# A softmax router on one core: eight-row loads in place of four-row loads for rows 4 to 35, and one float32 load for the first four rows

## The chip, the cores and the metric

The kernel runs on one core of a Trainium2 chip. The time is device microseconds of one execution; the time before is the median of seven runs. One further execution was taken by the hardware profiler, and every duration below comes from that one unless a text says otherwise.

## What is computed

```python
batch, seq, dim = 16, 512, 1024
num_loras = 8
# x: (16, 512, 1024) float32, router_weights: (1024, 8) float32
def reference(x, router_weights):
    logits = np.matmul(x, router_weights)
    exp_logits = np.exp(logits - np.max(logits, axis=-1, keepdims=True))
    return (exp_logits / np.sum(exp_logits, axis=-1, keepdims=True)).astype(np.float32)
```

There are 8,192 tokens. Each is multiplied by a 1024 x 8 matrix, and a softmax over eight numbers follows. The input is 33.6 MB, the output 0.26 MB.

## The kernel before, in words

The 8,192 tokens are laid over 128 partitions so that partition p holds 64 consecutive tokens (line 25 of the listing that follows). One "row" of the kernel is the j-th token of every partition: 128 tokens, 4 KB of float32 each. The 64 rows are worked off in order, and all of them stay in one bfloat16 buffer, `x_all` (`xa`), which has room for everything; no load waits for a buffer.

**Loads.** Rows 0 to 3 come as float32 into `x_f32` through SyncE's queue: two loads of two rows (line 134), each with a semaphore of its own, `s_f[0]` and `s_f[1]`. Rows 4 to 62 come through GpSimd's queue, which casts to bfloat16 on the way (line 185). The list `LOADS` (line 40) gives the rows of each: the first 4 is the float32 part, then twelve loads of four rows, three of two, five of one. The last row comes in three pieces of 4, 2 and 2 chunks of 128 columns (line 198). A load lays each partition's rows down as one contiguous run, so its packets hold one partition's rows: 16 KB of float32 read and 8 KB of bfloat16 written for four rows. GpSimd issues all of them at the start, one behind the other, and builds an identity matrix and a filler tile after the second (line 188). ScalarE's queue brings the weights (line 140).

**Handing rows on.** SyncE waits for the loads in order and counts their rows up in the semaphore `s_in` (lines 167 to 173). So a load's rows are available all at once, when the whole load is there.

**Work on one row.** TensorE transposes the row's eight 128 x 128 chunks against the identity into PSUM (line 293; the first row's at 248), five into `ptv` and three into `pts`. VectorE copies the five to SBUF (line 410), ScalarE the three (line 366). TensorE multiplies the chunks with the weights into `lg` (line 280). The loop (TensorE's bodies `rows_multiply` and `rows_turn`) turns row j + 1 before it multiplies row j, and puts two filler matmuls of 512 columns into every second row. Every eight rows VectorE and ScalarE do the softmax for a group (lines 430 to 452, 355).

**Start.** ScalarE waits for `s_f[0]`, casts rows 0 and 1 (`cast`, line 349), copies chunks for these rows, then waits for `s_f[1]`, casts rows 2 and 3 and copies their chunks. An activation table is loaded ahead of the first cast.

**End.** The last rows stand alone: rows 60 to 62 come out of single-row loads, row 63 in pieces (line 326), and after the last multiplication (line 340) follow one maximum, one exponential, a sum, a reciprocal, a scaling and the second output store (line 178). The first output store (line 176) goes out while the last pieces are still worked on.

Of the kernel before, what the change touches and what calls it, by code (L numbers as in the profile page):

```python
# [11 lines left out]
def kernel(  # L12
# [6 lines left out]
    nc = tc.nc  # L19
# [9 lines left out]
    x_rows = x.rearrange("b s d -> (b s) d").rearrange("(p j) d -> p j d", p=P)  # L29
# [7 lines left out]

    LOADS = [4] * 13 + [2, 2, 2] + [1] * 5  # L40
    PIECES = [4, 2, 2]
    G, SKIP = 8, 4
    TRIPS = 31
# [5 lines left out]
    DONE = ends[-2]  # L49
    assert sum(LOADS) == J - 1 and sum(PIECES) == KO and ends[-1] == J - ALONE  # L50
    VN, SN = 5, 3
# [3 lines left out]
    def sb(name, shape, dtype):  # L55
        size = mybir.dt.size(dtype)
        for n in shape[1:]:
            size *= n
        at = place[0]
        place[0] = -(-(at + size) // 64) * 64  # L60
        return nc.alloc_sbuf_tensor_at(name, shape, dtype, offset=at).ap()
# [5 lines left out]
    xa = sb("x_all", [P, J, D], bf16)  # L67
    x_f32 = sb("x_f32", [P, LOADS[0], D], fp32)
    identity = sb("identity", [P, P], bf16)
# [29 lines left out]
    sem = tc.alloc_semaphore  # L99


    s_f = [nc.alloc_semaphore(f"s_f{i}") for i in range(2)]
    s_w = nc.alloc_semaphore("s_w")
    s_ld = [sem(f"s_ld{i}") for i in range(len(LOADS))]
    s_z = [sem(f"s_z{i}") for i in range(len(PIECES))]
# [21 lines left out]

    first = [sum(LOADS[:i]) for i in range(len(LOADS))]
    cols = [sum(PIECES[:i]) for i in range(len(PIECES))]


    with tc.manual_schedule():
        early = [
            nc.sync.dma_start(
                out=x_f32[:, 2 * i:2 * i + 2, :], in_=x_rows[:, 2 * i:2 * i + 2, :]
            ).then_inc(s_f[i], 16)
            for i in range(2)
        ]
        early.append(
            nc.scalar.dma_start(  # L140
                out=w8, in_=router_weights.rearrange("(ko ki) n -> ko ki n", ko=KO)
            ).then_inc(s_w, 16)
        )
        for t in early:
            tc.no_tile_sem_insts.add(t.ins.name)
    tc.close()
# [19 lines left out]

    for j in range(LOADS[0]):
        sp.wait_ge(s_cast, j + 1)
        sp.sem_inc(s_in, 1)
    for i, r in enumerate(LOADS):  # L170
        if i:
# [11 lines left out]
    for i, r in enumerate(LOADS):  # L183
        if i:
            nc.gpsimd.dma_start(  # L185
                out=xa[:, first[i]:first[i] + r, :], in_=x_rows[:, first[i]:first[i] + r, :]
            ).then_inc(s_ld[i], 16)
        if i == 2:
# [3 lines left out]
                out=ident, in_=ident, compare_op=ALU.not_equal, fill=1.0, base=0,  # L192
# [154 lines left out]
    act = nc.scalar  # L347

    def cast(i):
        act.wait_ge(s_f[i], 16).then_inc(s_f[i], -16)  # L350
        for k in (2 * i, 2 * i + 1):
            act.copy(xa[:, k, :], x_f32[:, k, :]).then_inc(s_cast, 1)  # L352

# [9 lines left out]
    def act_copy(j, seen):  # L363

        act.wait_ge(s_ts, seen + 1)
        act.copy(xTs[j % 2], pts[j % 2][:, 0:SN, :]).then_inc(s_c[j % 2], 1)  # L366

    for i in range(2):
        cast(i)
        for j in (2 * i, 2 * i + 1):  # L370
            act_copy(j, j)
# [104 lines left out]
    with nc.body("dve_rows", valid_engines=only_dve):  # L476
# [42 lines left out]
        out=outv[:, J - ALONE:J, :], in0=ev3, in1=inv3.broadcast_to([P, ALONE, N]), op=ALU.mult  # L519
# [31 lines left out]
```

## Time and profile before

| | us |
|---|---|
| median of seven runs | 86.03 (85.86 to 86.48) |
| the profiled execution's own time | 85.89 |
| its span, first to last instruction | 84.6 |
| TensorE matmul busy | 63.2 (75%) |
| VectorE busy | 39.4 (47%) |
| ScalarE busy | 37.9 (45%) |
| DMA: bytes written | 18.12 MB, 3,904 packets |
| DMA: read from HBM | 33.59 MB, 400 GB/s over the span |
| GpSimd's queue, packets' time as a share of 16 engines' span | 91.0% |
| SyncE's queue, likewise | 7.5% |

The profile has a page of 40 equal slices (2.1 us each) with the busy share of each engine and of the DMA engines, a list of who waited for whom, the chain of work that ended last, a timeline of instructions, and tables by stretch. The trace under it also has a record for each DMA packet (start, duration, queue, bytes written) and for each landing (the sixteen semaphore increments of a load). "Busy" of a matmul is modelled and pipelined; queue engines (SPq, POOLq, PEq) are the sequencers that wait and issue. GB/s counts bytes written, so a float32-to-bfloat16 load at 215 GB/s reads 430 GB/s.

### The profile page before, as it was taken

How to read it: one execution, taken by the hardware profiler on the slowest of the kernel's cores; microseconds unless marked ns; L12 is line 12 of the kernel's file. 1: busy time of each engine (PE TensorE's matmuls, PEld its weight loads, DVE VectorE, ACT ScalarE, POOL GpSimd, SP SyncE). 2: the span in 40 equal slices, each digit the busy share in tenths (PEclk: the TensorE clock that was granted, in tenths of full speed). 3: DMA queues.
4: the chain of work that ended last, by engine and by line, in shares of the span. 5: the costliest groups of instructions: out<-in, count | busy, mean ns of one | idle time of the engine just before them, and what ended most of it. 6: DMA issues, size and time to landing. Idle time of an engine off the chain costs nothing. (4 is left out here: it accounts for less than half of the span.)

```text
span 84.6 us, 2926 instructions
## 1 busy us (share of the span) xinstructions
PE 63.2 (75%) x1094; PEld 51.9 (61%) x1094; DVE 39.4 (47%) x114; ACT 37.9 (45%) x81; POOL 13.4 (16%) x30
## 2 busy tenths in 40 slices
PE   0073759999895968959495986949497799999860
PEld 0043648888684747738384764837475588787650
DVE  0030422576472543834274452746256257665661
ACT  0049683366452442624254262535236246556470
POOL 0689999600000000000000000000000000000000
PEclk9999999999999999999999999999999999999998
DMA  5999999999999999999999999999999999999920
GB/s 107 417 426 260 221 202 225 205 229 205 213 217 213 221 213 221 205 229 205 221 213 221 209 225 202 232 202 225 205 225 190 215 217 213 201 210 208 180 102 23
DMA packets 3904, 18.12 MB, mean 214 GB/s; under 512 B 568, under 2 KB 1080, under 8 KB 2112
## 3 DMA queue, kind: packets, MB, share of 16 engines
q0 software_dynamic: 3312, 15.73, 91.0%
q1 hardware_dynamic: 576, 2.36, 7.5%
q10 hardware_dynamic: 16, 0.03, 0.1%
HBM read 33.59 MB, written 0.26 MB: 400 GB/s over the span
## 5 line engine op out<-in xcount | busy, mean ns | idle before, releaser
L366 ACT COPY xTs<-pts 128x384 bf16<-128x384 bf16 x63 | 30.0, 476 | 37.2 <-PE pts L293 36.8
L410 DVE COPY xTv<-ptv 128x640 bf16<-128x640 bf16 x63 | 30.9, 491 | 32.7 <-PE ptv L293 29.9
L293 PE MATMUL ptv<-identity,x_all 128*128 128x128 bf16 x311 | 28.5, 223 | 13.2 <-PEq L229 11.7
L293 PEld LDWEIGHTS ptv<-identity,x_all 128*128 (+1 forms) x311 | 18.7, 98 | 14.6 <-issue 14.5
L293 PE MATMUL pts<-identity,x_all 128*128 128x128 bf16 x186 | 21.3, 225 | 0.0
L280 PEld LDWEIGHTS lg<-w_bf,xTv 128*128 128x128 bf16 x305 | 15.5, 98 | 7.5 <-issue 0.8
L280 PE MATMUL spare<-filler 128*128 128x512 bf16 x61 | 19.2, 395 | 0.4
L280 PE MATMUL lg<-w_bf,xTv 128*128 128x8 bf16 x305 | 16.6, 167 | 0.0
L293 PEld LDWEIGHTS pts<-identity,x_all 128*128 x186 | 13.6, 101 | 0.0
L280 PE MATMUL lg<-w_bf,xTs 128*128 128x8 bf16 x183 | 13.2, 166 | 0.0
L185 POOL DMA_DIRECT2D x_all<-in_x_dram x20 | 10.7, 607 | 2.4 <-POOLq L147 2.4
L280 PEld LDWEIGHTS lg<-w_bf,xTs 128*128 128x128 bf16 x183 | 8.9, 96 | 0.0
L280 PEld LDWEIGHTS spare<-filler 128*128 128x128 bf16 x61 | 4.4, 101 | 2.5 <-issue 2.5
L287 PE MATMUL lg<-ident,w 8*128 8x8 f32 x8 | 1.0, 250 | 4.8 <-PEq L285 4.8
L352 ACT CAST x_all<-x_f 128x1024 bf16<-128x1024 f32 x4 | 4.0, 1045 | 0.0
L430 DVE TENSOR_REDUCE mx<-lg 128x8 f32 x8 | 1.8, 224 | 4.6 <-DVEq L480 4.1
L287 PEld LDWEIGHTS lg<-ident,w 8*128 8x128 f32 x8 | 0.9, 197 | 4.8 <-issue 4.8
L352 ACT ACT_TABLE_LOAD x1 | 1.3, 1283 | 5.3 <-ACTq L350 5.3
L355 ACT ACTIVATE ev<-ex 128x64 f32<-128x64 f32 x8 | 2.0, 256 | 1.6 <-DVE ex L430 0.9
L401 DVE CAST identity<-ident 128x128 bf16<-128x128 f32 x1 | 0.5, 518 | 4.8 <-POOL ident L191 4.8
L446 DVE TENSOR_REDUCE ssum<-ev 128x8 f32<-128x64 f32 x8 | 1.8, 220 | 0.1
L430 DVE TENSOR_TENSOR ex<-lg,mx 128x64 f32<-128x64 f32 x8 | 1.7, 216 | 0.0
(41 smaller groups left out, 16.0 us busy)
## 6 DMA issues: line engine op xcount, KB each, us to landing
x_all<-in_x_dram POOLq DMA_DIRECT2D x12, 1024.0 KB, 32.1
x_f<-in_x_dram SPq DMA_DIRECT2D x2, 1024.0 KB, 6.7
x_all<-in_x_dram POOLq DMA_DIRECT2D x3, 512.0 KB, 59.9
x_all<-in_x_dram POOLq DMA_DIRECT2D x5, 256.0 KB, 64.0
out_dram<-out_all SPq DMA_DIRECT2D x1, 208.0 KB, 1.9
x_all<-in_x_dram POOLq DMA_DIRECT2D x1, 128.0 KB, 65.6
x_all<-in_x_dram POOLq DMA_DIRECT2D x2, 64.0 KB, 65.4
out_dram<-out_all SPq DMA_DIRECT2D x1, 48.0 KB, 1.6
```

Source lines behind the costliest of these rows:

```text
L185: nc.gpsimd.dma_start(out=xa[:, first[i]:first[i] + r, :], in_=x_rows[:, first[i]:first[i] + r, :]).then_inc(s_ld[i], 16)
L280: return pe.matmul(spare, lhsT=filler[:, 0:P], rhs=filler, start=True, stop=True)
L287: t = pe.transpose(w_ps[:, n, :], w8[:, :, n], ident[0:KO, 0:KO])
L293: turn_like = pe.transpose(turn_ap(0, 0), xa[:, 0, 0:P], identity).ins
L352: act.copy(xa[:, k, :], x_f32[:, k, :]).then_inc(s_cast, 1)
L355: return act.activation(ev, ex, func=Exp).then_inc(s_ev, 1)
L366: act.copy(xTs[j % 2], pts[j % 2][:, 0:SN, :]).then_inc(s_c[j % 2], 1)
L401: dve.tensor_copy(out=identity, in_=ident).then_inc(s_idb, 1)
L410: dve.tensor_copy(out=xTv[j % 2], in_=ptv[j % 2][:, 0:VN, :]).then_inc(s_c[j % 2], 1)
L430: return dve.add_instruction(kind(name=f"I-{nc.next_id()}", engine=dve.engine, **k))
L446: dve.reduce_sum(ssum[:, :, 0], ev, axis=X).then_inc(s_d, 1)
```

## The change

`LOADS` becomes four, then four loads of eight rows, then four of four, and the tail as before. Rows 4 to 35 come in the loads of eight. The float32 part becomes one load of four rows with one semaphore `s_f`, and ScalarE waits for it once, ahead of the first cast, rather than once per pair of rows. The number of rows, the buffers, the order of the rows and every instruction of TensorE and VectorE stay. The order of the instructions on GpSimd stays too, with four loads fewer: the identity and the filler tile are still built after the second load.

```diff
-    LOADS = [4] * 13 + [2, 2, 2] + [1] * 5
+    LOADS = [4] + [8] * 4 + [4] * 4 + [2, 2, 2] + [1] * 5
...
-    s_f = [nc.alloc_semaphore(f"s_f{i}") for i in range(2)]
+    s_f = nc.alloc_semaphore("s_f")
...
         early = [
-            nc.sync.dma_start(
-                out=x_f32[:, 2 * i:2 * i + 2, :], in_=x_rows[:, 2 * i:2 * i + 2, :]
-            ).then_inc(s_f[i], 16)
-            for i in range(2)
-        ]
-        early.append(
+            nc.sync.dma_start(out=x_f32, in_=x_rows[:, 0:LOADS[0], :]).then_inc(s_f, 16),
             nc.scalar.dma_start(
                 out=w8, in_=router_weights.rearrange("(ko ki) n -> ko ki n", ko=KO)
-            ).then_inc(s_w, 16)
-        )
+            ).then_inc(s_w, 16),
+        ]
...
     def cast(i):
-        act.wait_ge(s_f[i], 16).then_inc(s_f[i], -16)
         for k in (2 * i, 2 * i + 1):
             act.copy(xa[:, k, :], x_f32[:, k, :]).then_inc(s_cast, 1)
...
+    act.wait_ge(s_f, 16).then_inc(s_f, -16)
     for i in range(2):
         cast(i)
```

## The prediction, as put on record

> **What bounds the kernel now.** I read the slices first, to see which resource is never idle.
>
> ```profile
> PE   0073759999895968959495986949497799999860
> ...
> DMA  5999999999999999999999999999999999999920
> GB/s 107 417 426 260 221 202 225 205 229 205 213 217 213 221 213 221 205 229 205 221 213 221 209 225 202 232 202 225 205 225 190 215 217 213 201 210 208 180 102 23
> ```
>
> The DMA engines are full from the second slice to about 80 us; TensorE has holes. The table by stretch gives the rate for the float32 loads, the four-row, two-row and one-row loads; its last column is GB/s written, and the cast loads read twice that.
>
> ```profile
> 2.50:6.50 4.00, 1.55 (x9) 1.05 (x9) 0.74 (x2) 1.18 (x1) 3.44 (x8) 1.00 1.01 425
> 12.29:65.86 53.57, 43.60 (x776) 35.56 (x774) 27.01 (x75) 22.87 (x52) 3.99 (x8) 1.00 1.03 215
> 65.86:73.24 7.38, 7.17 (x136) 6.04 (x136) 4.37 (x12) 3.59 (x9) 0.00 (x0) 1.00 1.06 211
> 73.24:79.49 6.25, 5.82 (x105) 4.64 (x102) 3.76 (x12) 3.13 (x8) 0.00 (x0) 1.00 1.13 207
> ```
>
> The rate falls as loads shrink: 215, 211, 207. That is the fixed price the change attacks, and it is small. Who waits confirms the bound: SyncE's list shows 66.6 us of waiting for loads in 19 waits, never over 4.9 us. TensorE's timeline shows the same between loads:
>
> ```profile
> 27.09 0.44 PE L293 MATMUL ptv<-identity,x_all 128*128 128x128 bf16 x5 [1.04 <-PEq L229]
> ...
> 28.39 0.44 PE L293 MATMUL ptv<-identity,x_all 128*128 128x128 bf16 x5
> ...
> 29.03 0.44 PE L293 MATMUL ptv<-identity,x_all 128*128 128x128 bf16 x5
> ...
> 30.11 0.44 PE L293 MATMUL ptv<-identity,x_all 128*128 128x128 bf16 x5
> ...
> 31.93 0.44 PE L293 MATMUL ptv<-identity,x_all 128*128 128x128 bf16 x5 [1.03 <-PEq L229]
> ```
>
> A four-row load every 4.84 us here, with 1.03 us of idle TensorE. Running freely, two rows take 1.72 us (28.39 to 30.11), so a row takes 0.86 us against 1.22 us of loading; a burst of four rows keeps TensorE busy for 4.84 - 1.03 = 3.8 us. The chain that ended last is the tail behind the last pieces:
>
> ```profile
> 79.66 0.44 PE ptv L293 x5
> ...
> 80.97 0.21 PE extra L326 x2
> ...
> 81.43 0.36 PE lg L340 x8
> ...
> 82.74 0.19 DVE out_all L518
> ```
>
> By the landing records the last piece is there at 80.85 and its transposes start at 80.97; the span ends 3.71 us after that landing. So the time is: start of the load stream, plus its work, plus 3.7 us of tail, plus 85.89 - 84.56 = 1.33 us around the span. I make the sum on this execution's 85.89, which lies 0.14 under the median of 86.03.
>
> **Part 1: four eight-row loads for eight four-row loads.** Landings of the four-row loads run from 12.29 to 65.86 in 11 steps, 4.870 each. Two-row loads: (73.24 - 65.86)/3 = 2.460. One-row loads: (79.49 - 73.24)/5 = 1.250. Two two-row loads cost 0.050 more than one of four; four one-row loads cost 0.130 more, 0.043 for each load too many. The packet records say the same by another way: on an engine, packets of 16, 8 and 4 KB read follow each other every 0.606, 0.305 and 0.154 us, so joining two 8 KB packets saves 2 x 0.305 - 0.606 = 0.004, eight packets an engine per load make 0.032, and one semaphore packet less is worth 0.017 to 0.021: 0.05. The trace has no 32 KB packet; the nearest row is the joining of 8 KB into 16 KB. I take 0.05 a load: four loads fewer, **-0.20 us**; bounds -0.16 (0.04 each, as the one-row loads say) and, should the packet's fixed share not shrink any further, -0.08 (semaphore packets alone).
>
> The Trainium skill, page "DMA: Bandwidth & Descriptors", section on the anatomy of one DMA on the GpSimd path, fits a DMA's time as about 2.0 us plus bytes over 436e3. If that fixed part stood in line, five DMAs fewer would save an estimated 10 us; this trace's 4.870 against 2 x 2.460 shows that queued loads hide all but 0.05 of it.
>
> **Part 2: one float32 load.** Its packets (8 KB, every 0.306 us) grow to 16 KB: eight joins of 0.004 and one semaphore packet of 0.006, 0.04 us an engine. It counts only on engines still busy with float32 when GpSimd's first packets arrive, at 6.54 us. Five engines finished between 6.54 and 6.63 and would merely idle; but two engines (last float32 packets at 7.26 and 7.42) are late, and a load lands with its slowest engine (11.77 to 12.29 for the first). So **-0.04 us**, bounds 0 and, below, -0.35: the first packets took 0.39 to 1.13 us instead of 0.31 and five second ones 0.57 to 0.74, and if the surcharge went by packet, half the packets would spare a late engine about 0.35 (0.66 - 0.31). I read the slow first 1.2 us as a matter of time, not of packets, since all recover together near 2.2 us, and take 0 for it.
>
> **Part 3: ScalarE waits for all four rows.** Before, `s_f[0]` landed at 5.22:
>
> ```profile
> 5.32 1.28 ACT L352 ACT_TABLE_LOAD   x1 [5.32 <-ACTq L350]
> 6.62 1.99 ACT L352 CAST x_all<-x_f 128x1024 bf16<-128x1024 f32 x2
> 8.99 0.48 ACT L366 COPY xTs<-pts 128x384 bf16<-128x384 bf16 x1 [0.39 <-PE pts L248]
> ```
>
> The second load landed only at 8.66, because from 6.54 the queues take turns packet by packet: the latest engine shows 0.62 (GpSimd), 0.32 (float32), 0.62 (GpSimd), then its semaphore packet. With GpSimd's packets twice as long (1.21 us) the joined load lands at about 7.1 + 1.2 + 0.3 = 8.6; if one data packet is still caught behind GpSimd's, near 9.9. The table load sits behind the wait, so the first cast starts at 9.9 to 11.2, not 6.62: everything on rows 0 to 3 comes 3.3 to 4.6 us later. Queued behind that wait on ScalarE are the table load, the casts and the copies of rows 0 to 3; SyncE waits for the casts before it counts any later row, and TensorE waits for SyncE. Row 4 was turned at 14.43, so it could be at 17.7 to 19.0. But the first eight-row load lands only at 12.29 + 4.82 = 17.1. So 0.6 to 1.9 us of lateness remain. Later landings are at 26.8, 36.5 and 46.2; a cold eight rows at 2.6 us a pair (11.45 to 16.01, matmuls at 314 ns) still end before 29.5, and warm ones gain it back. Cost **0**, hidden by the loads.
>
> **Part 4: coarser hand-over.** Row 35 is available at 46.2 as before (46.38 less the savings), but now with rows 28 to 34: TensorE is done with them at 46.2 + 0.2 (from landing to first transpose) + 3.8 + 4 x 0.86 = 53.6. Rows 36 to 39 end at 57.1, 40 to 43 at 60.5, and the next load lands at 60.8: caught up one load later. From there on everything is as before. Cost **0**; the cover is the 0.35 us a row by which TensorE is faster, over 27 rows.
>
> The idle hole of TensorE grows from 1.03 to 9.69 - 3.8 - 4 x 0.86 = 2.4 us. Here a rule speaks against the change: the page "TensorE: Matmul & The Clock Gate", section "Why this matters for your kernels", wants no gap over about 3 us, or the clock halves. The 1.03-us holes in this trace cost nothing (matmuls at 218 ns after them); no row shows 2.4 us. By that rule an estimate of the sum stays at -0.24, since 2.4 is under 3.
>
> Whatever the limit is, the trace prices it: cold rows take 1.30 us, 0.44 more. If all eight rows 28 to 35 were cold, 3.5 us would be lost, rows would run on TensorE's pace to the end, and row 62 would be turned some 0.2 to 0.4 us late, which about eats the gain.
>
> **Sum:** -0.20 - 0.04 = -0.24: 85.65 for an execution like the profiled one, 86.03 - 0.24 = **85.79** as a median.
>
> **Rivals.**
> 1. *32 KB packets run slower* (the one that ends slower). Four loads have 32 of them on each engine, 38.7 us; each per cent costs 0.39 us, the gain is gone at 0.6%. For it: between 9 and 12 us, while GpSimd issued, 16 KB packets took up to 0.651 instead of 0.625 (4%). Against it: per-packet time is straight from 4 to 16 KB. At 2%: 86.56. Chance 0.12.
> 2. *TensorE goes cold in the longer holes*, as priced: about 86.1. Chance 0.03.
> 3. *It does not do what it says*: 32 KB are cut into 16 KB packets, or the fixed share does not shrink; only semaphore packets go: -0.08, 85.95. Chance 0.10.
> 4. *The start gains too*: -0.24 - 0.3, 85.5. For it: the slow first packets. Chance 0.12.
> 5. The forecast, 85.79, own range 85.6 to 85.95: chance 0.63.
>
> **Numbers.** A measurement here tells about 0.3% (0.26 us) from no change. The forecast sits on that line; its unknown ends reach further down than up, so I split it 0.36 faster, 0.27 same. Faster 0.36 + 0.12 = 0.48; same 0.27 + 0.03 + 0.10 = 0.40; slower 0.12. The range leaves out rival 1 and a little of rival 4: 85.45 to 86.2.
>
> **What the profile after must show.** GpSimd's queue with 2,736 packets (19 loads and pieces of 8 + 1 packets on 16 engines) instead of 3,312; first casts at 9.9 to 11.2; TensorE holes near 2.4 us before 46 us and 218-ns matmuls after them; landings of eight rows every 9.69; row 44's load found by an idle TensorE; the last piece at 80.6. I am wrong if 32 KB packets follow each other at more than 1.22 us, if TensorE never idles again after 46 us, or if the first cast load lands later than 17.3.

## The result and the profile after

| | before | after |
|---|---|---|
| median, us | 85.99 (85.74 to 86.48, 76 runs) | 85.71 (85.59 to 85.95, 30 runs) |
| ratio, 95% interval | | 0.9969 (0.9961 to 0.9976) |
| profiled execution, us | 85.89 | 85.83 |
| its span, us | 84.6 | 84.5 |
| last piece landed, us | 80.85 | 80.83 |

The change makes the kernel 0.28 us faster, 0.31%; the interval is 0.21 to 0.34 us. It was forecast at 0.24 us: 85.79 against 86.03. The two profiled executions differ by only 0.06 us. In the one of after, rows 8 to 11 were there at 17.26 us, against 17.16 before, although one load had been saved by then. So the gain has to be read between landings, not in the two spans.

The slices of the page of after: the first line is the granted clock, then the DMA engines' busy share and what they wrote.

```profile
PEclk9999999999999999955589999999999999999998
DMA  5999969997999799989998999999998999999920
GB/s 140 411 450 256 233 140 248 240 225 155 248 240 225 155 248 240 202 178 248 240 202 175 213 221 209 225 194 240 190 244 184 217 215 213 200 208 210 168 102 23
...
q0 software_dynamic: 2736, 15.73, 90.2%
...
x_all<-in_x_dram POOLq DMA_DIRECT2D x4, 2048.0 KB, 27.6
```

The load stream is as full as before: on an engine the 32 KB packets follow each other every 1.208 us at the median without a gap, and the dips to 140 or 155 GB/s come from counting such a long packet in the slice in which it starts. GpSimd's queue carries 2,736 packets, as forecast, so the 32 KB packets exist. New are the three slices at half clock near 40 us. Who SyncE waited for (total us, times, longest), before and after, and then ScalarE's start after:

```profile
SPq L173 <- DMA x_all<-in_x_dram: 66.6, 19, 4.9
```

```profile
SPq L168 <- DMA x_all<-in_x_dram: 63.5, 16, 9.7
```

```profile
8.51 1.28 ACT L346 ACT_TABLE_LOAD   x1 [8.51 <-ACTq L362]
9.81 1.99 ACT L346 CAST x_all<-x_f 128x1024 bf16<-128x1024 f32 x2
```

The longest wait for a load is now 9.7 us, a load of eight. ScalarE starts its casts at 9.81 instead of 6.62. TensorE's timeline of after shows the hand-over; in brackets stands how long TensorE was idle before:

```profile
27.11 0.44 PE L288 MATMUL ptv<-identity,x_all 128*128 128x128 bf16 x5 [1.79 <-PEq L224]
...
36.86 0.69 PE L288 MATMUL ptv<-identity,x_all 128*128 128x128 bf16 x5 [2.49 <-PEq L224]
...
61.15 0.44 PE L288 MATMUL ptv<-identity,x_all 128*128 128x128 bf16 x5 [0.45 <-PEq L224]
```

After a hole of 2.49 us the five transposes take 0.69 us instead of 0.44: the granted clock is half from 36.08 to 42.90 us. After the hole of 1.79 us they take 0.44. Ahead of rows 36 and 40 (51 and 56 us) there is no hole at all, TensorE is behind. At 61.15 it waits again, which is rows 44 to 47: caught up. The chain that ended last is the one of before, 0.03 us earlier:

```profile
79.63 0.44 PE ptv L288 x5
...
80.94 0.21 PE extra L321 x2
...
82.72 0.19 DVE out_all L513
```

### The profile page after: what moved, and what is told of

Same layout as the page of the kernel before. It is cut to its first block, busy times and chain, and to the rows that moved or that the text cites. A ratio compares the mean times of both kernels' runs of the same rounds, so it can differ in the third digit from the quotient of the medians.

```text
span 84.5 us, 2916 instructions
## 1 busy us (share of the span) xinstructions
PE 64.1 (76%) x1094; PEld 53.4 (63%) x1094; DVE 39.4 (47%) x114; ACT 38.1 (45%) x81; POOL 11.3 (13%) x26
## 3 DMA queue, kind: packets, MB, share of 16 engines
q0 software_dynamic: 2736, 15.73, 90.2%
## 5 line engine op out<-in xcount | busy, mean ns | idle before, releaser
L288 PE MATMUL ptv<-identity,x_all 128*128 128x128 bf16 x311 | 29.6, 229 | 12.6 <-PEq L224 7.6
L288 PEld LDWEIGHTS ptv<-identity,x_all 128*128 (+1 forms) x311 | 19.3, 101 | 13.6 <-issue 13.6
L288 PE MATMUL pts<-identity,x_all 128*128 128x128 bf16 x186 | 22.1, 231 | 0.0
L275 PEld LDWEIGHTS lg<-w_bf,xTv 128*128 128x128 bf16 x305 | 16.0, 99 | 8.3 <-issue 1.9
L275 PE MATMUL spare<-filler 128*128 128x512 bf16 x61 | 20.2, 414 | 0.2
L288 PEld LDWEIGHTS pts<-identity,x_all 128*128 x186 | 14.2, 105 | 0.0
L180 POOL DMA_DIRECT2D x_all<-in_x_dram x16 | 8.6, 592 | 2.2 <-POOLq L142 2.2
```

Source lines behind the costliest of these rows:

```text
L180: nc.gpsimd.dma_start(out=xa[:, first[i]:first[i] + r, :], in_=x_rows[:, first[i]:first[i] + r, :]).then_inc(s_ld[i], 16)
L275: return pe.matmul(spare, lhsT=filler[:, 0:P], rhs=filler, start=True, stop=True)
L288: turn_like = pe.transpose(turn_ap(0, 0), xa[:, 0, 0:P], identity).ins
```

## The experiments

Theory A is that of the prediction: each load in GpSimd's queue has a fixed price of about 0.05 us, the end is set by the load stream alone, and everything later in the first 60 us is covered. The rivals put the gain at the start (B), in semaphore packets alone (C), or in the two parts together (D). A hole is idle time of TensorE ahead of a load's rows.

**Eight-row loads alone**, run twice.

```diff
-    LOADS = [4] * 13 + [2, 2, 2] + [1] * 5
+    LOADS = [4] + [8] * 4 + [4] * 4 + [2, 2, 2] + [1] * 5
```

> The four eight-row loads alone; the float32 part stays in two loads. Theory A (each load in the queue has a fixed price of about 0.05 us): four loads fewer, 0.20 us faster than before, 85.79 against 85.99, ratio 0.9977; the eight-row loads land every 9.69 to 9.70. Rival B (the gain of 0.28 sits at the start, in the one float32 load): no change, within 0.05 us. Rival C (only the semaphore packets go): 0.08 faster, ratio 0.9991.

Measured: 85.73 against 85.86, ratio 0.9985 (0.9969 to 1.0002). By its landings the eight-row loads came every 9.69 us ((46.06 - 16.99)/3). The interval held both A and nothing, so the kernel ran once more, beside the whole change:

> The eight-row loads alone once more, since the first interval (0.9969 to 1.0002) held both 0.20 us and nothing. Theory A: ratio 0.9977, and within 0.05 us of the whole change. Theory D: 0.1 us or more behind the whole change.

> The changed kernel unaltered, on the same chip as its parts. Theory A: 0.20 to 0.24 us faster than before, ratio 0.9972 to 0.9977. If the two parts together give more than their sum (theory D: the float32 load matters only beside longer GpSimd packets), this is clearly faster than the eight-row loads alone in the same call, by 0.1 us or more.

Measured beside each other: the loads alone 85.78 against 85.91, ratio 0.9979 (0.9969 to 0.9989); the whole change 85.76, ratio 0.9982 (0.9972 to 0.9991). The loads alone do what the whole change does, so B falls. The medians of the two differ by 0.02 us, the means by 0.01 with an interval of about 0.10 to both sides, so the 0.1 us of D lies at the edge of what these runs exclude. The whole change, forecast here at 0.20 to 0.24 us, came out at 0.15 us, with an interval of 0.08 to 0.24.

**The one float32 load alone**: the diff of the change without its first edit, here seen from the changed kernel.

```diff
-    LOADS = [4] + [8] * 4 + [4] * 4 + [2, 2, 2] + [1] * 5
+    LOADS = [4] * 13 + [2, 2, 2] + [1] * 5
```

> The one float32 load alone; rows 4 to 35 stay in eight loads of four. Theory A: 0.04 us faster than before at most (ratio 0.9995), first cast at about 9 us since GpSimd's packets of 16 KB hold the last float32 packets up by 0.6 and not by 1.2. Rival B: 0.2 to 0.28 faster, ratio 0.997.

Measured: 85.89 against 85.86, ratio 1.0008 (0.9994 to 1.0021). The 0.04 us of the prediction is just inside the interval, a gain of 0.2 is not. Its float32 load landed at 7.98 and its first cast began at 9.38, where about 9 was expected. In the seven other profiled executions with one float32 load, where GpSimd's packets in between are of 32 KB and not of 16, that load landed at 8.33 to 8.49.

**More loads instead of fewer**: rows 4 to 35 in sixteen loads of two, and in thirty-two of one.

```diff
-    LOADS = [4] * 13 + [2, 2, 2] + [1] * 5
+    LOADS = [4] + [2] * 16 + [4] * 4 + [2, 2, 2] + [1] * 5
```

> Rows 4 to 35 in sixteen loads of two rows, the rest as before: eight loads more than before. Theory A: 8 x 0.05 = 0.40 us slower, ratio 1.0047. Rival B: no change. Rival C (a semaphore packet of 0.02 a load and nothing else): 0.16 slower, ratio 1.0019.

Measured: 86.26 against 85.86, ratio 1.0052 (1.0028 to 1.0075), 0.45 us for eight loads, 0.056 each.

```diff
-    LOADS = [4] * 13 + [2, 2, 2] + [1] * 5
+    LOADS = [4] + [1] * 32 + [4] * 4 + [2, 2, 2] + [1] * 5
```

> Rows 4 to 35 in thirty-two loads of one row: twenty-four loads more than before. Theory A from the one-row loads of the tail (0.043 to 0.05 a load): 1.04 to 1.2 us slower, ratio 1.012 to 1.014. Rival C (semaphore packets alone, 0.02): 0.48 slower, ratio 1.0056.

Measured: 87.12 against 85.91, ratio 1.0144 (1.0129 to 1.0158), 1.24 us for twenty-four loads, 0.052 each. C is far outside. In every one of these kernels a load has eight data packets and one semaphore packet on each engine, so the runs price a load with its packets and do not tell the two apart. The DMA view of the one-row kernel has the longer queue:

```profile
q0 software_dynamic: 6768, 15.73, 95.4%
```

**Eight-row loads up to row 51**, where the tail leaves no time to catch up.

```diff
-    LOADS = [4] + [8] * 4 + [4] * 4 + [2, 2, 2] + [1] * 5
+    LOADS = [4] + [8] * 6 + [2, 2, 2] + [1] * 5
```

> As the changed kernel, but rows 36 to 51 come in two eight-row loads too, two loads fewer again. By theory A's price the load stream ends another 0.10 us earlier. But rows 44 to 51 are handed over together at 65.6; TensorE at 0.86 us a row is done with them at 73.0 and with row 62 at 82.5 where before had it at 80.3: 2.2 us slower than before, 88.2, if the clock stays up, and up to 3.5 more if it is halved in the hole ahead of that load. If the hand-over cost nothing (a theory that only bytes and loads count), it would be 0.30 faster than before, 85.69.

Measured: 88.18 against 85.86, ratio 1.0263 (1.0217 to 1.0309). The last piece landed at 80.64, 0.2 us earlier than before, and the kernel is 2.3 us slower. Its four times lie between 87.78 and 89.38, the longest with the lowest mean granted clock (0.916 against 0.950 to 0.961); the profiled execution took 87.93. The chain that ended last tells why; before it was 21 pieces from 79.6 us on, here 84 from 65.82 on, and its first lines are:

```profile
65.82 0.44 PE ptv L288 x5
66.46 0.60 PE spare L275 x2
67.07 0.18 PE lg L275 x8
67.25 0.30 PE ptv L288 x5
```

From the landing of rows 44 to 51 to 81.1 us nothing but TensorE's own work stands in the chain; then the last group's softmax and ScalarE's copies follow. Row 62 is turned at 81.57 instead of 79.66, and a load that ends earlier is worth nothing. The granted clock was full from 60.88 us to the end of TensorE's work, so this profiled execution shows the coarser hand-over alone. It had half clock from 57.47 to 60.88, and was through with those rows before the next load.

**Eight-row loads up to row 43**, one load fewer than the changed kernel.

```diff
-    LOADS = [4] + [8] * 4 + [4] * 4 + [2, 2, 2] + [1] * 5
+    LOADS = [4] + [8] * 5 + [4] * 2 + [2, 2, 2] + [1] * 5
```

> Rows 36 to 43 in an eight-row load as well, rows 44 to 51 in two of four: one load fewer than the changed kernel. Theory A: another 0.05 us, 0.25 to 0.29 faster than before, ratio 0.9967 to 0.9971. TensorE is handed rows 36 to 43 at 55.9 and is done at 63.1, at 70.0 with row 51 and back in step with the loads only at row 62, so there is no cover left: with the clock halved in the hole ahead of that load it would end up to 1.7 us later, 87.7.

Measured: median 86.07 against 85.91, ratio 1.0023 (0.9998 to 1.0047), but the twelve times fall into two heaps: six from 85.62 to 85.88, six from 86.25 to 87.73. The profiled one, 85.64, showed full clock after 56 us. Three more profiled executions of the same kernel were to show what a long one does:

> The kernel with eight-row loads to row 43 again, one profiled execution; its twelve times spread from 85.6 to 87.7 where the others spread by 0.4. Theory K (the clock halves in the hole ahead of rows 36 to 43, in some executions and not in others, and there is no cover left behind it): an execution under 85.9 shows 0.44-us groups of five transposes after 56 us and row 62 turned at 79.5 to 79.7; one over 86.2 shows 0.69-us groups there for 2 to 4 us, 1 to 2 us lost, and row 62 turned as late as the execution is long. Rival L (the load stream itself is later in the long executions): the last piece lands later than 80.9 in them.

> As the look before it: by theory K the last piece lands at 80.6 to 80.9 in every execution, long or short, and a long one has its half-clock stretch after 56 us; by rival L the last piece lands later in a long one.

> A third execution of the same kernel, read as the two before it: theory K puts the lost time into half-clock groups of 0.69 us after 56 us, rival L into a later last landing.

Measured: 86.23, 85.72 and 85.71 (one execution of before beside them: 86.24). The last piece landed at 80.65, 80.68 and 80.67, so the loads are alike and rival L falls. The table by stretch, 56 to 61 us, of the first of the three and of the second; the column before the DMA share is the granted clock:

```profile
56.00:61.00 5.00, 4.89 (x70) 4.13 (x71) 2.21 (x7) 1.73 (x5) 0.00 (x0) 0.67 1.03 215
```

```profile
56.00:61.00 5.00, 4.83 (x89) 3.98 (x90) 3.24 (x10) 2.54 (x6) 0.00 (x0) 1.00 1.01 211
```

The long execution got 70 matmuls done in five us, the short one 89. The timeline of the long one, rows 36 to 38 and 62:

```profile
56.11 0.69 PE L288 MATMUL ptv<-identity,x_all 128*128 128x128 bf16 x5 [2.39 <-PEq L224]
...
58.02 0.69 PE L288 MATMUL ptv<-identity,x_all 128*128 128x128 bf16 x5
59.09 0.54 PE L288 MATMUL ptv<-identity,x_all 128*128 128x128 bf16 x5
```

```profile
79.26 0.44 PE L288 MATMUL ptv<-identity,x_all 128*128 128x128 bf16 x5
79.91 0.44 PE L288 MATMUL ptv<-identity,x_all 128*128 128x128 bf16 x5
```

Row 62 is turned at 79.91 without a wait, where the short ones turn it at 79.55 and 79.56 after waiting for its load. Here is the second of the three:

```profile
79.56 0.44 PE L288 MATMUL ptv<-identity,x_all 128*128 128x128 bf16 x5 [0.47 <-PEq L224]
```

The long one's span is 0.52 us longer than the second's: 0.35 by row 62, and the rest by ScalarE's copies behind it, which then stand in the chain. The third had half clock from 45.88 to 49.30 us, on rows 28 and 29, and was a short one: there the rows that follow cover it. Theory K stands for these profiles: a half-clock stretch with too little cover behind it is paid. Row 44 came 1.1 us later than in the second execution (64.37 us against 63.25), of the 1 to 2 expected, and 0.5 us of that reached the end. The other long executions, 86.25 to 87.73, were not profiled in full. The mean granted clock is on record for each: 0.933 to 0.957 in the six long ones, 0.967 to 0.980 in four of the short ones and 0.933 in the other two. So the long ones had much half clock, but where it lay is not shown, and that they are the same thing is argued. This variant has the shortest single executions but not the better median; none of the variants beats the changed kernel.

## Why the prediction was right, point by point

**Part 1, -0.20: right, and all of the gain that the runs can place.** Within profiles, eight-row loads land every 9.688 us (five steps, 17.21 to 65.65, in the kernel with eight rows up to row 51) against 2 x 4.870 before: 0.052 saved per load dropped, where the prediction took 0.05. The same rows in these two profiles, 48.44 us against 48.70:

```profile
17.21:65.65 48.44, 40.06 (x691) 33.50 (x689) 23.98 (x66) 20.49 (x46) 0.00 (x0) 0.93 1.01 215
```

```profile
17.16:65.86 48.70, 38.73 (x708) 31.57 (x705) 24.82 (x69) 20.95 (x48) 0.00 (x0) 1.00 1.03 215
```

Over the nine profiled executions with eight-row loads the step is 9.67 to 9.71 us (9.70 in after), 0.03 to 0.07 saved per load. The packet records of after have 32 KB packets every 1.208 us at the median, just 2 x 0.606 - 0.004. In the other direction the price was 0.052 and 0.056 a load. As a time the four loads were worth 0.13 and 0.18 us in two runs (by the ratios; 0.13 both times by the medians), with intervals that hold 0.20. The prediction's estimate of 10 us counts the fixed part for five loads, but the fifth load dropped is SyncE's and not on the GpSimd path; by its own working it is 8 us, and the argument against it stays.

**Part 2, -0.04: this term is not seen.** The float32 load alone gave +0.07 us, interval -0.05 to +0.18. Its packets do follow each other every 0.607 us instead of 2 x 0.306, but the stream's start takes as long: by 6 us 1.76 MB had been read before, 1.76 with the float32 load alone and 1.78 after. That the slow start goes by time and not by packets (where the prediction took 0 against -0.35) was right; rival 4 falls.

**The sum, -0.24: in part luck.** The main comparison gave 0.28 us (0.21 to 0.34) and the second run of the same kernel 0.15 (0.08 to 0.24). The shown price of the loads, 0.20, lies between the two. No experiment says what makes 0.28 of it in one comparison and 0.15 in the other; the median of before alone was 85.99, 85.86 and 85.91 in the three comparisons. That the forecast came within 0.04 us of the first is no evidence for its last hundredths.

**Part 3, cost 0: right.** The joined load was there at 8.42 (predicted 8.6), the first cast began at 9.81 (9.9 to 11.2), the first eight-row load landed at 17.26 (17.1). In the second run of the eight-row loads alone the second float32 load was so unlucky in taking turns with the 32 KB packets (last data packets at 9.35 to 9.41 us, semaphore packets at 10.9) that it landed at 11.26, and that execution took 85.84 us: still hidden.

**Part 4, cost 0: right, with its cover.** In after, TensorE was back in step at rows 44 to 47, as worked out; in the second profiled execution of the changed kernel, which had half clock on rows 28 and 29, one load later, at rows 48 to 51. The kernel with eight rows up to row 51 took that cover away and came out at 88.18, expected 88.2. So close a meeting is partly luck, since its four times spread by 1.6 us. Its profile measures the pace: rows 44 to 62 were turned from 65.82 to 81.57, 0.875 us a row, where the prediction took 0.86.

**Where a step failed:** "By that rule an estimate of the sum stays at -0.24, since 2.4 is under 3", and the list of what must show, "218-ns matmuls after them". The holes came nearly as forecast: in the changed kernel's two profiles 1.79 and 1.86 us ahead of row 12, 2.48 and 2.49 ahead of row 20, and 2.41 ahead of row 28 in the one that had no half clock just before. But after 10 of the 14 holes of 2.38 to 2.49 us in all profiles the clock was halved. The measurement decides against the rule of the Trainium skill's page "TensorE: Matmul & The Clock Gate" (section "Why this matters for your kernels": no gaps over about 3 us).

**Rival 2** (TensorE goes cold, that is to half clock, in the longer holes; chance 0.03, 86.1) had its condition come true and its price not. It priced eight cold rows at 0.44 us each, 3.5 us. Measured, the clock came back after 3.41 or 6.83 us, before eight rows were through. In after the half clock lay on rows 20 to 23 and was over before rows 28 to 35 were there: nothing was lost. In the second profiled execution of the changed kernel (85.69 us) it began at 45.83 us, on row 28:

```profile
46.37 0.69 PE L288 MATMUL ptv<-identity,x_all 128*128 128x128 bf16 x5 [2.41 <-PEq L224]
...
54.53 0.44 PE L288 MATMUL ptv<-identity,x_all 128*128 128x128 bf16 x5
...
65.84 0.44 PE L288 MATMUL ptv<-identity,x_all 128*128 128x128 bf16 x5 [0.81 <-PEq L224]
...
79.47 0.44 PE L288 MATMUL ptv<-identity,x_all 128*128 128x128 bf16 x5 [0.40 <-PEq L224]
```

From row 28 to row 36 (the second line) it took 8.16 us, against 7.12 in after (46.53 to 53.65): 1.04 us lost, and made good by row 48 (the third line). Row 62 (the last) waits for its load as ever. So the forecast was right in spite of this step: the cover of Part 4 was there, and the half clock was shorter than the price had assumed, which nothing in the prediction had worked out.

**Rival 1** (32 KB packets slower) falls: they follow each other every 1.208 us at the median, 1.21 in the mean; only between 7 and 12 us, while GpSimd issued, was it 1.233. **Rival 3** falls with the packet count and the dose. The last piece was forecast at 80.6 and landed at 80.83 in the profiled execution, at 80.68 in the one beside the parts.

## What to carry to other kernels

These are lessons of one kernel. When the DMA queue is never empty, a load's price is the gap it adds between landings: measure it from loads of two sizes in the same trace (here 0.05 us a load), not from a load by itself. Larger loads then pay that little back, and they are free only as long as the consumer can catch up before the stream ends: count the rows behind the last large load times the consumer's spare time per row, and compare it with the burst plus a half-clock stretch. Put large loads early and let them shrink towards the end.

## What the runs showed of the hardware

**The clock goes by a grid, not by the hole alone.** In thirteen profiles the granted clock changes only at steps of 3.41 us from its first rise: it lasts, for example, 10.24, 17.07 or 27.31 us at full and 3.41 or 6.83 at half, all multiples. Laid over TensorE's holes, every change to half between that rise and the last rows follows a grid window in which holes make 1.66 us or more (after: window 32.66 to 36.08, hole from 34.37), and windows with up to 1.62 us left it up: a hole of 2.74 us that a grid line cut into 1.22 and 1.52 cost nothing, one of 1.91 us with 1.66 in one window halved the clock. The same 2.4-us hole therefore halves the clock in one execution and not in the next. That this spreads the times of the kernel with eight rows up to row 43 is seen in its four profiled executions and argued for the others. Idleness in the window is not the whole rule: the clock also falls after the last multiplication, and there it followed windows with only 1.1 to 1.4 us of idleness in four profiles. So the limit of nearly half a window holds for this kernel's middle, is read from these traces and was not tried by itself.

**The scatter is there by the first eight-row landing.** The same kernel (eight-row loads alone) had read 1.85 MB by 6 us in one profile and 1.72 in the other; at 0.43 MB a microsecond that is 0.31 us. Its first eight-row loads landed at 16.99 and 17.32, and the two executions took 85.53 and 85.84. The changed kernel's two profiles had read 1.78 and 1.76 MB by 6 us, yet landed these rows at 17.26 and 17.08 and took 85.83 and 85.69: there the difference came between 6 and 17 us. Differences of 0.2 us between two single profiles of this kernel mean nothing; the steps between landings within each do.
